# Seven-product SwiGLU in a hybrid decoder layer: weight sums moved to VectorE, rounds overlapped by one product

## The chip, the cores and the metric

The kernel runs on one core of one Trainium2 chip. The metric is the device time of one execution in microseconds, taken as the median of several runs. The engines are named as in the profile: PE is TensorE's matmul, PEld its weight load, DVE is VectorE, ACT is ScalarE, POOL is GpSimd, SP is SyncE, which here only issues DMAs.

## The reference

One decoder layer on 512 tokens of width 1024, in float32: three token mixers (a gated linear recurrence, a chunked gated linear attention, a complex diagonal state space model), merged and projected; cross-attention into 256 memory tokens; a SwiGLU feed-forward of width 2816; a layer norm after each. The change touches the last part:

```
h2 = LN2(alpha * h1 + xattn)
gate, up = split(h2 @ w_gu)               # 1024 x 5632
h3 = LN3(alpha * h2 + (silu(gate) * up) @ w_down)
```

## The kernel before

Every weight product is made in a split form. A block of weights (128x1024, float32) is loaded by SP into a raw tile, copied by ACT to a rounded tile `whi`, and DVE writes the remainder `wlo = raw - whi`. The activations are split likewise into a high and a low part, and `mm3` (L439) runs three matmuls per pair: high by high, high by low, low by high.

All weight blocks stand in one list, `order`, and four functions walk along it. `dma_to` (L251) issues loads, `hi_to` (L303) ACT's copies, `split_to` (L322) DVE's remainders, and `take` (L351) hands the next block to the product. `take` of block i first emits the remainder of block i+3 and ACT's copy of block i+4; loads are emitted with the copy, or up to three blocks ahead where `room` (L341) finds space. These blocks, sums and split halves share a pool of 14 buffers (`W`, tag "w"); a new tile takes a buffer that came free longest ago, and its writer waits on the chip for the last reader of that buffer. Each engine runs its own instructions strictly in the order in which the program emits them; between engines semaphores order the work.

The feed-forward's first product has 22 features of 128 columns. The first four are plain products of gate and up. Of these the first four blocks are begun on tokens 0 to 255 alone (`half_plain`, L1614), since the transposed tiles of tokens 256 to 511 come later from LN2. The other 18 features are made in nine rounds of two features (L1713). A round treats the weights as a 2x2 block matrix (11, 12, 21, 22: halves of the inner dimension by gate and up), the activations as another (halves of the inner dimension by halves of the tokens), and makes the four block products with seven products instead of eight, for which sums of weight blocks (t1 = 12 - 11, t2 = 22 - t1, 22 - 12, t4 = 21 - t2) and sums of activation blocks (s1 to s4) are needed. One `product` (L1701) is 24 matmuls of 256 columns.

`factor` (L263) loads the four blocks of a round and makes the four weight sums on POOL as `dma_to` reaches them. The seven products of a round run in the order 11, 12, s2, s1, s3, s4, 22 (named by their activation block) and collect in three PSUM banks: pb takes 11, then s2 on top, then s3, then 22; pc takes s1, then s4; pa takes 12. Between them ACT copies bank contents out (m1, u2, m5) and DVE adds (m1 += pa, m5 += pb, u2 += pc). The results sg and sh are queued in `late` and split into `act` tiles by `act_split` (L1660).

The activation sums s1 to s4 are made in `h2_T` (L1591), which a token tile of LN2 calls once its transposes are queued: four 128x512 instructions on POOL for each of tiles 2 and 3. LN2's own power (the inverse root, in `ln_apply`, L485) stands in the same POOL queue. `place_s3` (L1691) writes the split s3 over the tokens' block 21 after the second product of the first round.

The down product is `proj_ln` (L1413) on 11 units for each half of the columns. Its residual h2, stored to DRAM before, is loaded again by `load_res` (L1485) with eight DMAs from POOL's queue, ahead of the call; the LN3 parameters follow with four more in its first unit.

Of the kernel before, what the change touches and what calls it, by code (L numbers as in the profile page):

```python
# [9 lines left out]
F32 = mybir.dt.float32  # L10
# [148 lines left out]
def hybrid_kernel(ctx: ExitStack, tc: tile.TileContext, I, out, dbg=None):  # L159
# [80 lines left out]
    add("w_xq", 8)  # L240
    add("w_xo", 8)
    add("w_gu", 2 * NPLAIN)
    for d in range((KF - NPLAIN) // 2):
        for n in range(7):
            order.append(("w_gu", (NPLAIN + 2 * d, n), 1024))
    add("w_dn", KF)
    raws, splits = {}, {}
    blk = {}
# [2 lines left out]
    def dma_to(n):  # L251
        while st["dma"] < min(n, len(order)):
            i = st["dma"]
            st["dma"] += 1
            name, j, size = order[i]
            if type(j) is tuple:
                raws[i] = factor(*j)
                continue
            size = min(size, I[name].shape[2])
            raws[i] = W("raw", F32)  # L260
            SP.dma_start(raws[i][:, :size], I[name][j])

    def factor(f, n):  # L263


        b = blk.setdefault(f, {})

        def load(k):

            h, up = ((0, 0), (0, 1), (1, 1), (1, 0))[k]  # L270
            b[k] = W("raw", F32)
            for e in range(2):
                SP.dma_start(b[k][:, 512 * e:512 * e + 512], I["w_gu"][2 * (f + e) + up][:, 512 * h:512 * h + 512])

        if n == 0:
            load(0)
            return b[0]
        if n == 1:
            load(3)
            return b[3]  # L280
        if n == 2:
            load(1)
            load(2)
            b["t1"], b["t2"] = W("t1", F32), W("t2", F32)
            G.tensor_tensor(b["t1"], b[1], b[0], ALU.subtract)
            G.tensor_tensor(b["t2"], b[2], b["t1"], ALU.subtract)
            del b[0]
            return b["t2"]
        if n == 3:
            return b.pop("t1")  # L290
        if n == 4:
            G.tensor_tensor(b[1], b[2], b[1], ALU.subtract)
            return b.pop(1)
        if n == 5:
            return b.pop(2)
        t = W("t4", F32)
        G.tensor_tensor(t, b[3], b["t2"], ALU.subtract)
        del blk[f]
        return t

# [2 lines left out]
    def hi_to(n):  # L303

        while st["hi"] < min(n, len(order)):
            i = st["hi"]
            dma_to(i + 1)
            st["hi"] += 1
            if i < NK32:
                continue  # L310
            name, _, size = order[i]
            if name == "w_lr":
                pair = W("wlr", F32R)
                p3 = pair[:, :size].rearrange("p (k e c) -> p e k c", e=2, c=16)
                r3 = raws.pop(i)[:, :size // 2].rearrange("p (k c) -> p k c", c=16)
                his[i] = (p3[:, 0], p3[:, 1], r3, pair)
            else:
                hi = W("whi", F32R)
                his[i] = (hi[:, :size], None, raws.pop(i)[:, :size], hi)
            A.activation(his[i][0], his[i][2], AF.Copy)  # L320
# [19 lines left out]

    def room():  # L341

        names = {x.name for b in blk.values() for x in b.values()} | {x.name for x in raws.values()}
        names |= {x[2].name for x in his.values()}
        return 2 * max(keep[0], 1) + 2 * len(splits) + len(his) + len(names) + 2 <= NBUF_W

# [1066 lines left out]
    def proj_ln(name, actT, nk, hres, lnj, outT, final=False, need=None):  # L1413

        nu = nk // 2
        last = min(4, nu)

        def part(pss, un, w, ts, stop):  # L1420
            for kk in range(2):
                k = 2 * un + kk
                if need is not None:
                    need(k)
                for t in ts:
                    mm3(pss[t], actT[k][t] if type(actT[k]) is list else cut(actT[k], ALL, slice(t * P, (t + 1) * P)),
                        cut(w, ALL, slice(kk * 512, kk * 512 + 512)), k == 0, stop and k == nk - 1)

        sts = [S("st", 7) for _ in range(NT)]

        def half(t, c, ps):
            V.scalar_tensor_tensor(hres[t][c], hres[t][c], ALPHA, ps, ALU.mult, ALU.add,
                                   accum_out=sts[t][:, c:c + 1])
            if c == 0:
                ln_first(hres[t][0], sts[t])

        first = [PS("p0") for _ in range(NT)]
        for un in range(nu):
            w = take(name)
            part(first, un, w, range(NT), True)  # L1440
            if un == 0:
                gb = ln_params(lnj)
            slot()
        second = [PS("p1") for _ in range(NT)]
        done = 0
        for un in range(nu - last):
            w = take(name)
            part(second, un, w, range(NT), False)
            if done < NT:
                half(done, 0, first[done])  # L1450
                done += 1
            slot()
        while done < NT:
            half(done, 0, first[done])
            done += 1
        ws = [take(name, min(AHEAD, NPAIR - 1 - un)) for un in range(last)]
        hout, es = [None] * NT, []

        def tile_gen(t):
            h = ln_apply(hres[t], sts[t], gb)  # L1460
            hout[t] = h
            if final:
                for c in range(2):
                    SP.dma_start(out[t * P:(t + 1) * P, c * 512:(c + 1) * 512], h[c])
                return
            yield T, h[0], h[1]
            if callable(outT):
                outT(h, t)
            else:
                ln_T(h, t, outT)  # L1470
            yield 0

        for t in range(NT):
            for un in range(last):
                part(second, nu - last + un, ws[un], [t], True)
                if t == NT - 1:
                    split_to(nxt[0] + min(AHEAD, NPAIR - last + un + 1))
                if un == 0 and t > 1:
                    finish(es[t - 2])
            half(t, 1, second[t])  # L1480
            es.append(start_bg(tile_gen(t)))
            slot()
        return hout, es
# [107 lines left out]
    def h2_T(h, t):  # L1591
        plain[t] = [H("hT0"), H("hT1")]
        for c in range(2):
# [3 lines left out]
            dst = (ALL, ALL, slice(t * P, (t + 1) * P))  # L1597
            split(h2T8[0][c][dst], h2T8[1][c][dst], ps.rearrange("p (k t) -> p k t", t=P))
            A.activation(plain[t][c], ps, AF.Copy)
        if t < 2:  # L1600
            return

        (a11, a12), (a21, a22) = plain[t - 2], plain[t]
        G.tensor_tensor(a22, a21, a22, ALU.add)
        G.tensor_tensor(a21, a11, a21, ALU.subtract)
        G.tensor_tensor(a11, a22, a11, ALU.subtract)
        G.tensor_tensor(a12, a12, a11, ALU.subtract)
        sums[t] = {"s1": a22, "s2": a11, "s3": a21, "s4": a12}

    h2, es = proj_ln("w_xo", oT, KD, h1, 2, h2_T, need=need_head)  # L1610
    finish_all(es[0], es[1])
# [19 lines left out]
        place("s4", part, H("s4", F32R), H("s4", F32R))  # L1631
    for i, (w, ps) in enumerate(pre):
        half_plain(ps, w, 1)
        if i < 3:
            for t in (2, 3):
                n = ("s2", "s1", "s4")[i]
                to_block(n, t, sums[t][n])
        keep[0] -= 1
        split_to(nxt[0] + min(AHEAD, i + 1))
        prefetch(st["split"] + DMA_AHEAD)  # L1640
# [50 lines left out]
    def place_s3():  # L1691
# [1 line left out]
        for part in range(2):  # L1693
            pl["s3", part], wr["s3", part] = pl["21", part], wr["21", part]
        for t in (2, 3):
            to_block("s3", t, sums[t]["s3"])
        sums.clear()
        plain.clear()

# [10 lines left out]
        product(ps, take("w_gu"), n, first)  # L1710
        slot()

    for d in range((KF - NPLAIN) // 2):  # L1713
        pa, pb, pc_ = PS("wa"), PS("wb"), PS("wc")
        m1, m5, u2, sg, sh = H("m1"), H("m5"), H("u2"), H("sg"), H("sh")
        step(pb, "11", True)
        A.activation(m1, pb, AF.Copy)
        step(pa, "12", True)
        V.tensor_tensor(m1, pa, m1, ALU.add)
        A.activation(sg, m1, AF.Silu)  # L1720
        if d == 0:
            place_s3()
        step(pb, "s2")
        A.activation(u2, pb, AF.Copy)
        step(pc_, "s1", True)
        A.activation(m5, pc_, AF.Copy)
        step(pb, "s3")
        V.tensor_tensor(m5, pb, m5, ALU.add)
        step(pc_, "s4")
        V.tensor_tensor(u2, pc_, u2, ALU.add)  # L1730
        V.tensor_tensor(sg, sg, u2, ALU.mult)
        step(pb, "22")
        A.activation(sh, pb, AF.Silu)
        V.tensor_tensor(sh, sh, m5, ALU.mult)
        fs = [NPLAIN + 2 * d, NPLAIN + 2 * d + 1]
        act_tiles(fs, (0, 1), sg)
        act_tiles(fs, (2, 3), sh)
        if len(late) > 9:
            act_split()
        del m1, m5, u2, sg, sh, pa, pb, pc_  # L1740
    pl.clear()
    wr.clear()

# [1 line left out]
        while late and (act[min(k + 6, KF - 1)] is None or None in act[min(k + 6, KF - 1)]):  # L1745
            act_split()

    hres = load_res(h2d)
    hout, es = proj_ln("w_dn", act, KF, hres, 3, None, final=True, need=need_act)
    finish_all(*es)  # L1750
    assert nxt[0] == len(order)
    LOG.append(("life", plan.life))
# [90 lines left out]
```

## Time and profile before

| | |
|---|---|
| median of 3 runs | 1017.77 us (1017.7 to 1022.61) |
| the profiled execution | 1021.16 us, its span 1019.5 us |
| PE busy | 981.0 us, 96% |
| PEld busy | 840.3 us, 82% |
| DVE busy | 633.9 us, 62% |
| ACT busy | 417.1 us, 41% |
| POOL busy | 288.9 us, 28% |
| mean granted clock of TensorE | 0.989 of full |

Times in the rows are microseconds from the span's start, or nanoseconds where a mean or median of one instruction is given. PE's busy time counts pipelined instructions and is not a measure of its peak; what counts here is when it stands idle and where its clock falls. The rounds of the seven-product form run from 687.27 to 891.43 us, the down product follows.

### The profile page before, as it was taken

The page shows a single profiled execution, that of the slowest core. Times are in us where ns is not written, and L with a number is a line of the kernel's source. Part 1 is how long each engine was busy: PE and PEld are TensorE (multiplying, and loading weights), DVE is VectorE, ACT ScalarE, POOL GpSimd, SP SyncE. Part 2 cuts the span into 40 slices and gives each one's busy share as a digit, 9 for nine tenths or more (in the row PEclk, how much of TensorE's full clock was granted, in tenths as well). Part 3 has the DMA queues.
Part 4 walks back from the last instruction along what each step waited for, and adds up shares of the span by engine and source line. Part 5 has one row for each costly group of instructions (what it writes and reads, how often), then busy time and mean ns, then how long its engine had stood idle before and what let it go on. Part 6 is the DMA issues. An engine that isn't in the chain of part 4 may idle for free. (4 is left out here: it accounts for less than half of the span.)

```text
span 1019.5 us, 14088 instructions
## 1 busy us (share of the span) xinstructions
PE 981.0 (96%) x5504; PEld 840.3 (82%) x5504; DVE 633.9 (62%) x935; ACT 417.1 (41%) x672; POOL 288.9 (28%) x325
## 2 busy tenths in 40 slices
PE   9999999999999999999989999899989999799996
PEld 7888778877888888888878887889989899788885
DVE  5725897695686634575854557657777776653316
ACT  5634565523343225533534443444344434442311
POOL 1489950053315010020100001544444454400001
PEclk9999999999999999999989999899999999999998
DMA  9932132324245454372321212142233322632202
GB/s 352 338 124 101 62 118 100 108 84 134 94 126 184 134 165 145 120 237 97 124 83 63 102 63 82 46 142 84 83 111 115 108 83 84 248 125 86 101 21 82
DMA packets 43554, 123.85 MB, mean 121 GB/s; under 512 B 5440, under 2 KB 5856, under 8 KB 43488
## 3 DMA queue, kind: packets, MB, share of 16 engines
q1 hardware_dynamic: 35040, 97.79, 27.8%
q0 software_dynamic: 6592, 22.02, 6.6%
q10 hardware_dynamic: 1856, 3.15, 1.1%
q8 instruction: 43, 0.70, 0.3%
q14 instruction: 23, 0.19, 0.1%
HBM read 109.31 MB, written 11.53 MB: 119 GB/s over the span
## 5 line engine op out<-in xcount | busy, mean ns | idle before, releaser
L75 DVE TENSOR_TENSOR wlo<-raw,whi 128x1024 fp32r<-128x1024 f32 x162 | 206.4, 1282 | 89.8 <-PE p L75 45.6
L75 ACT ACTIVATE whi<-raw 128x1024 fp32r<-128x1024 f32 x162 | 170.0, 1058 | 109.4 <-PE p L75 34.3
L75 PE MATMUL p<-whi,act 128*128 128x512 f32 x352 | 108.6, 389 | 0.0
L75 POOL TENSOR_TENSOR st<-st,mh 128x1 f32<-128x1 f32 x16 | 15.1, 946 | 267.7 <-DVE st L75 267.7
L75 PE MATMUL gt<-h0Th,whi 128*128 128x512 f32 x192 | 79.2, 413 | 0.0
L75 PEld LDWEIGHTS p<-whi,act 128*128 128x128 f32 x352 | 66.1, 188 | 13.7
L75 PE MATMUL gt<-h0Th,wlo 128*128 128x512 f32 x192 | 75.0, 391 | 0.0
L75 PE MATMUL gt<-h0Tl,whi 128*128 128x512 f32 x192 | 74.9, 390 | 0.0
L75 DVE TENSOR_TENSOR wlo<-t,whi 128x1024 fp32r<-128x1024 f32 x27 | 52.2, 1934 | 31.8 <-ACT whi L75 31.8
L75 PE MATMUL wb<-h2Th,whi 128*128 128x256 f32 x216 | 61.9, 287 | 7.9 <-ACT u L75 7.9
L75 PE MATMUL p<-wlo,act 128*128 128x512 f32 x176 | 68.5, 389 | 0.0
L75 PE MATMUL wb<-h2Tl,whi 128*128 128x256 f32 x216 | 61.1, 283 | 0.0
L75 PE MATMUL wb<-h2Th,wlo 128*128 128x256 f32 x216 | 61.1, 283 | 0.0
L75 PE MATMUL wc<-s,whi 128*128 128x256 f32 x288 | 53.9, 287 | 3.7 <-ACT m L75 3.7
L75 ACT ACTIVATE th<-gt,gbh 128x512 f32<-128x512 f32 x24 | 16.6, 692 | 98.4 <-PE gt L75 89.4
L75 POOL TENSOR_TENSOR t<-raw,t 128x1024 f32<-128x1024 f32 x18 | 49.8, 2766 | 21.4 <-issue 14.5
L75 ACT ACTIVATE whi<-t 128x1024 fp32r<-128x1024 f32 x27 | 27.6, 1049 | 63.8 <-POOL t L75 63.8
L75 PEld LDWEIGHTS wb<-h2Th,whi 128*128 128x128 f32 x216 | 41.4, 191 | 9.5 <-ACT u L75 9.5
L75 PEld LDWEIGHTS wc<-s,whi 128*128 128x128 f32 x288 | 45.6, 195 | 3.9 <-ACT m L75 3.9
L75 POOL TENSOR_TENSOR t<-raw,raw 128x1024 f32<-128x1024 f32 x9 | 21.6, 2403 | 91.9 <-DMA raw<-in_w_gu 39.2
L75 PE MATMUL wc<-s,wlo 128*128 128x256 f32 x144 | 41.7, 289 | 1.2 <-DVE wlo L75 1.2
L75 PEld LDWEIGHTS gt<-h0Th,wlo 128*128 128x128 f32 x192 | 36.0, 188 | 7.7
(393 smaller groups left out, 2576.0 us busy)
## 6 DMA issues: line engine op xcount, KB each, us to landing
raw<-in_w_gu SPq DMA_DIRECT2D x72, 256.0 KB, 3.9
raw<-in_w_dn SPq DMA_DIRECT2D x22, 512.0 KB, 3.5
raw<-in_w_xk SPq DMA_DIRECT2D x8, 512.0 KB, 6.7
raw<-in_w_gatea SPq DMA_DIRECT2D x8, 512.0 KB, 3.5
raw<-in_w_gateb SPq DMA_DIRECT2D x8, 512.0 KB, 3.5
raw<-in_w_gatec SPq DMA_DIRECT2D x8, 512.0 KB, 4.3
raw<-in_w_xv SPq DMA_DIRECT2D x8, 512.0 KB, 3.5
raw<-in_w_mix SPq DMA_DIRECT2D x8, 512.0 KB, 3.7
```

The costliest lines, as they stand in the source:

```text
L75: return f(*a, **k)
```

## The change

- The weight sums and the activation sums are made on DVE (`V`) in place of POOL (`G`).
- Loading and summing are parted. `load_blocks` issues the loads when `dma_to` reaches a block; `factor` makes the sums only when `hi_to` reaches it, just ahead of ACT's copy.
- The order of a round becomes 11, 22 of the round before, s2, s1, 12, s3, s4; the last "22" follows the loop (`last_product`). The loads go in the order 11, then 12 and 22 together, then 21. The bank pb and the tile m5 of a round live on into the next.
- The activation sums are no longer made in `h2_T` but by `sum_of`, behind the second halves of the first and third plain blocks.
- `place_s3` stands behind the first product of the first round.
- `act_split` is called in the last four rounds (before: from the third round on, in seven of nine).
- The last residual is loaded inside `proj_ln`, in the second unit of its first half.

```diff
     add("w_gu", 2 * NPLAIN)
-    for d in range((KF - NPLAIN) // 2):
-        for n in range(7):
-            order.append(("w_gu", (NPLAIN + 2 * d, n), 1024))
+    fs = range(NPLAIN, KF, 2)
+    for f in fs:
+        order += [("w_gu", (g, n), 1024) for g, n in ((f, 1), (f - 2, 4), (f, 6), (f, 5), (f, 2), (f, 7), (f, 3))
+                  if g >= NPLAIN]
+    order.append(("w_gu", (fs[-1], 4), 1024))
...
-    def factor(f, n):
+    def load_blocks(f, n):
         b = blk.setdefault(f, {})
+        for k in {1: ("11",), 6: ("12", "22"), 2: ("21",)}.get(n, ()):
             b[k] = W("raw", F32)
+            h, up = int(k[0]) - 1, int(k[1]) - 1
             for e in range(2):
                 SP.dma_start(b[k][:, 512 * e:512 * e + 512], I["w_gu"][2 * (f + e) + up][:, 512 * h:512 * h + 512])
...
+    def factor(f, n):
+        b = blk[f]
+        if n < 4:
+            return b["11" if n == 1 else "21" if n == 2 else "22"]
+        if n == 6:
             b["t1"], b["t2"] = W("t1", F32), W("t2", F32)
-            G.tensor_tensor(b["t1"], b[1], b[0], ALU.subtract)
-            G.tensor_tensor(b["t2"], b[2], b["t1"], ALU.subtract)
+            V.tensor_tensor(b["t1"], b["12"], b["11"], ALU.subtract)
+            V.tensor_tensor(b["t2"], b["22"], b["t1"], ALU.subtract)
...
-            G.tensor_tensor(b[1], b[2], b[1], ALU.subtract)
+            V.tensor_tensor(b["12"], b["22"], b["12"], ALU.subtract)
...
-        G.tensor_tensor(t, b[3], b["t2"], ALU.subtract)
+        V.tensor_tensor(t, b["21"], b["t2"], ALU.subtract)
...
             if un == 0:
                 gb = ln_params(lnj)
+            if un == 1 and callable(hres):
+                hres = hres()
...
-        G.tensor_tensor(a22, a21, a22, ALU.add)
-        G.tensor_tensor(a21, a11, a21, ALU.subtract)
-        G.tensor_tensor(a11, a22, a11, ALU.subtract)
-        G.tensor_tensor(a12, a12, a11, ALU.subtract)
+    def sum_of(n, t):
+        (a11, a12), (a21, a22) = plain[t - 2], plain[t]
+        o, x, y, op = {"s1": (a22, a21, a22, ALU.add), "s3": (a21, a11, a21, ALU.subtract),
+                       "s2": (a11, a22, a11, ALU.subtract), "s4": (a12, a12, a11, ALU.subtract)}[n]
+        V.tensor_tensor(o, x, y, op)
...
+    def last_product(f, pb, m5):
+        step(pb, "22")
+        sh = H("sh")
+        A.activation(sh, pb, AF.Silu)
+        V.tensor_tensor(sh, sh, m5, ALU.mult)
+        act_tiles([f, f + 1], (2, 3), sh)
+
+    before = None
+    for f in range(NPLAIN, KF, 2):
         step(pb, "11", True)
         A.activation(m1, pb, AF.Copy)
-        step(pa, "12", True)
-        V.tensor_tensor(m1, pa, m1, ALU.add)
-        A.activation(sg, m1, AF.Silu)
-        if d == 0:
+        if before is None:
             place_s3()
+        else:
+            last_product(*before)
         step(pb, "s2")
         A.activation(u2, pb, AF.Copy)
         step(pc_, "s1", True)
         A.activation(m5, pc_, AF.Copy)
+        step(pa, "12", True)
+        V.tensor_tensor(m1, pa, m1, ALU.add)
+        A.activation(sg, m1, AF.Silu)
         step(pb, "s3")
         V.tensor_tensor(m5, pb, m5, ALU.add)
         step(pc_, "s4")
...
-        if len(late) > 9:
+        act_tiles([f, f + 1], (0, 1), sg)
+        before = (f, pb, m5)
+        if f >= KF - 8:
             act_split()
...
+    last_product(*before)
...
-    hres = load_res(h2d)
-    hout, es = proj_ln("w_dn", act, KF, hres, 3, None, final=True, need=need_act)
+    hout, es = proj_ln("w_dn", act, KF, lambda: load_res(h2d), 3, None, final=True, need=need_act)
```

## Rows read from the trace of the kernel before

**Rows 1.** The page, its head: the span of the profiled execution.
```profile
span 1019.5 us, 14088 instructions
```

**Rows 2.** Stretches: us, busy of each engine (instructions), PEclk, DMA share, GB/s.
```profile
631.59:652.21 20.62, 14.81 (x113) 13.93 (x111) 13.62 (x22) 7.99 (x13) 6.33 (x5) 0.91 0.30 100
652.21:665.48 13.27, 13.12 (x97) 12.83 (x97) 9.51 (x12) 8.13 (x16) 9.55 (x12) 0.88 0.34 121
687.27:707.30 20.03, 20.03 (x170) 20.03 (x169) 13.90 (x13) 8.20 (x11) 7.32 (x3) 1.00 0.32 106
749.95:772.50 22.55, 20.85 (x171) 20.24 (x170) 16.49 (x13) 10.06 (x13) 10.21 (x5) 1.00 0.29 94
863.00:891.43 28.43, 22.54 (x171) 21.72 (x169) 16.70 (x15) 12.18 (x15) 13.95 (x15) 0.94 0.61 221
687.27:891.43 204.16, 187.44 (x1514) 183.15 (x1512) 146.10 (x116) 89.87 (x115) 91.66 (x45) 0.99 0.34 114
```

**Rows 3.** Waits of PE, 687 to 892 us: waited for, total us, times, longest.
```profile
PE wb L75 <- ACT u L75: 7.9, 8, 1.1
PE wb L75 <- ACT m L75: 4.0, 6, 1.0
PE wc L75 <- ACT m L75: 3.7, 1, 3.7
```

**Rows 4.** The chain of waits, 736 to 760 us: start, us, what.
```profile
740.22 0.33 SPq L75
...
742.49 5.32 DMA raw<-in_w_gu
...
752.99 1.99 DVE wlo L75
```

**Rows 5.** Instructions of single tiles in the loop: duration ns min/median/max, first and last start.
```profile
L75 DVE TENSOR_TENSOR wlo<-raw,whi x37: 1207/1224/3416, 689.5 to 890.1; 128x1024 fp32r<-128x1024 f32 x37
L75 DVE TENSOR_TENSOR wlo<-t,whi x26: 1210/1227/3426, 688.1 to 876.8; 128x1024 fp32r<-128x1024 f32 x26
...
L75 POOL TENSOR_TENSOR t<-raw,t x17: 2407/2733/3264, 690.8 to 869.1; 128x1024 f32<-128x1024 f32 x17
```

**Rows 6.** Groups by form in the loop: busy us, mean ns | idle before, releaser.
```profile
L75 DVE TENSOR_TENSOR wlo<-t,whi 128x1024 fp32r<-128x1024 f32 x26 | 49.9, 1919 | 28.4 <-ACT whi L75 28.4
...
L75 ACT ACTIVATE whi<-raw 128x1024 fp32r<-128x1024 f32 x38 | 40.1, 1056 | 23.0 <-DMA raw<-in_w_gu 10.6 <-DMA raw<-in_w_dn 7.6 <-issue 2.8
...
L75 DVE TENSOR_TENSOR sh<-sh,m 128x512 f32<-128x512 f32 x8 | 5.4, 678 | 0.0
L75 ACT ACTIVATE u<-wb 128x512 f32<-128x512 f32 x9 | 5.2, 577 | 0.0
```

**Rows 7.** The chain of waits at the end of LN2.
```profile
642.95 1.68 POOL hT L75
...
649.00 0.52 POOL st L75
649.54 0.76 DVE lh L75
```

**Rows 8.** The timeline of PE there: start, us, instruction, idle before.
```profile
650.44 1.09 PE L75 MATMUL tp<-ident,lh 128*128 128x128 f32 x4 [4.11 <-DVE lh L75]
```

**Rows 9.** Instructions on the LN statistics, 637 to 660 us.
```profile
L75 DVE TENSOR_TENSOR st<-st x4: 149/702/1267, 642.2 to 644.7; 128x1 f32<-128x1 f32 x4
...
L75 DVE SCALAR_TENSOR_TENSOR st<-st x1: 159/159/159, 646.0 to 646.0; 128x1 f32<-128x1 f32 x1
```

**Rows 10.** The page, DMA issues: KB each, median us to landing.
```profile
raw<-in_w_gu SPq DMA_DIRECT2D x72, 256.0 KB, 3.9
```

**Rows 11.** DMA issues from 860 to 900 us: KB each, median us to landing.
```profile
raw<-in_w_dn SPq DMA_DIRECT2D x8, 512.0 KB, 8.8
res<-h2d POOLq DMA_DIRECT2D x8, 256.0 KB, 6.8
```

**Rows 12.** The residual's first use, from 860 us on.
```profile
L75 DVE SCALAR_TENSOR_TENSOR res<-res,p x7: 679/686/687, 949.5 to 1005.9; 128x512 f32<-128x512 f32 x7
```

More of the change, by code (lines that the diff above doesn't have):

```diff
@@ L256, in dma_to @@
             if type(j) is tuple:
-                raws[i] = factor(*j)
+                load_blocks(*j)
+                raws[i] = None
                 continue
@@ L261, in dma_to @@
             SP.dma_start(raws[i][:, :size], I[name][j])
-    def factor(f, n):
+    def load_blocks(f, n):
         b = blk.setdefault(f, {})
-        def load(k):
-            h, up = ((0, 0), (0, 1), (1, 1), (1, 0))[k]
+        for k in {1: ("11",), 6: ("12", "22"), 2: ("21",)}.get(n, ()):
             b[k] = W("raw", F32)
+            h, up = int(k[0]) - 1, int(k[1]) - 1
             for e in range(2):
                 SP.dma_start(b[k][:, 512 * e:512 * e + 512], I["w_gu"][2 * (f + e) + up][:, 512 * h:512 * h + 512])
[L275 to L283, printed above, removed]
+    def factor(f, n):
[3 more added lines that the diff above has]
+        if n == 6:
             b["t1"], b["t2"] = W("t1", F32), W("t2", F32)
-            G.tensor_tensor(b["t1"], b[1], b[0], ALU.subtract)
-            G.tensor_tensor(b["t2"], b[2], b["t1"], ALU.subtract)
-            del b[0]
+            V.tensor_tensor(b["t1"], b["12"], b["11"], ALU.subtract)
+            V.tensor_tensor(b["t2"], b["22"], b["t1"], ALU.subtract)
+            del b["11"]
             return b["t2"]
-        if n == 3:
+        if n == 5:
             return b.pop("t1")
-        if n == 4:
-            G.tensor_tensor(b[1], b[2], b[1], ALU.subtract)
-            return b.pop(1)
-        if n == 5:
-            return b.pop(2)
+        if n == 7:
+            V.tensor_tensor(b["12"], b["22"], b["12"], ALU.subtract)
+            return b.pop("12")
         t = W("t4", F32)
-        G.tensor_tensor(t, b[3], b["t2"], ALU.subtract)
+        V.tensor_tensor(t, b["21"], b["t2"], ALU.subtract)
         del blk[f]
@@ L310, in hi_to @@
                 continue
-            name, _, size = order[i]
+            name, j, size = order[i]
+            if type(j) is tuple:
+                raws[i] = factor(*j)
             if name == "w_lr":
@@ L341, in room @@
     def room():
-        names = {x.name for b in blk.values() for x in b.values()} | {x.name for x in raws.values()}
+        names = {x.name for x in (*raws.values(), *(t for b in blk.values() for t in b.values())) if x is not None}
         names |= {x[2].name for x in his.values()}
@@ L1599, in h2_T @@
             A.activation(plain[t][c], ps, AF.Copy)
-        if t < 2:
-            return
+    def sum_of(n, t):
         (a11, a12), (a21, a22) = plain[t - 2], plain[t]
-        G.tensor_tensor(a22, a21, a22, ALU.add)
-        G.tensor_tensor(a21, a11, a21, ALU.subtract)
-        G.tensor_tensor(a11, a22, a11, ALU.subtract)
-        G.tensor_tensor(a12, a12, a11, ALU.subtract)
-        sums[t] = {"s1": a22, "s2": a11, "s3": a21, "s4": a12}
+        o, x, y, op = {"s1": (a22, a21, a22, ALU.add), "s3": (a21, a11, a21, ALU.subtract),
+                       "s2": (a11, a22, a11, ALU.subtract), "s4": (a12, a12, a11, ALU.subtract)}[n]
+        V.tensor_tensor(o, x, y, op)
+        sums[n, t] = o
     h2, es = proj_ln("w_xo", oT, KD, h1, 2, h2_T, need=need_head)
@@ L1633, in hybrid_kernel @@
         half_plain(ps, w, 1)
-        if i < 3:
-            for t in (2, 3):
+        for t in (2, 3):
+            for n in (("s1", "s3", "s2"), (), ("s4",), ())[i]:
+                sum_of(n, t)
+            if i < 3:
                 n = ("s2", "s1", "s4")[i]
-                to_block(n, t, sums[t][n])
+                to_block(n, t, sums[n, t])
         keep[0] -= 1
@@ L1695, in place_s3 @@
         for t in (2, 3):
-            to_block("s3", t, sums[t]["s3"])
+            to_block("s3", t, sums["s3", t])
         sums.clear()
@@ L1711, in step @@
         slot()
-    for d in range((KF - NPLAIN) // 2):
+    def last_product(f, pb, m5):
[6 more added lines that the diff above has]
+    for f in range(NPLAIN, KF, 2):
         pa, pb, pc_ = PS("wa"), PS("wb"), PS("wc")
-        m1, m5, u2, sg, sh = H("m1"), H("m5"), H("u2"), H("sg"), H("sh")
+        m1, m5, u2, sg = H("m1"), H("m5"), H("u2"), H("sg")
         step(pb, "11", True)
         A.activation(m1, pb, AF.Copy)
-        step(pa, "12", True)
-        V.tensor_tensor(m1, pa, m1, ALU.add)
-        A.activation(sg, m1, AF.Silu)
-        if d == 0:
+        if before is None:
             place_s3()
+        else:
+            last_product(*before)
         step(pb, "s2")
@@ L1731, in hybrid_kernel @@
         V.tensor_tensor(sg, sg, u2, ALU.mult)
[L1732 to L1737, printed above, removed]
-        if len(late) > 9:
+        act_tiles([f, f + 1], (0, 1), sg)
+        before = (f, pb, m5)
+        if f >= KF - 8:
             act_split()
-        del m1, m5, u2, sg, sh, pa, pb, pc_
+    last_product(*before)
     pl.clear()
```

## The prediction

> **What bounds the kernel now.** I read the page first: the span is 1019.5 us [rows 1], and TensorE is busy nearly all of it, so every microsecond to win is one in which TensorE stands still or runs at its lower clock. The table of stretches [rows 2] says where that is. The loop of the seven-product form lasts 204.16 us (687.27 to 891.43). Its first round takes 20.03 us with TensorE never idle, which is 2.86 us for each of the seven products. Nine such rounds would be 180.3 us, so 23.9 us of the loop are lost; the last round alone takes 28.43 us, at a granted clock of 0.94. The second place is the end of LN2: 631.59 to 652.21 and the stretch after it, with clocks of 0.91 and 0.88.
>
> TensorE's waits in the loop [rows 3] name ACT copies out of PSUM. But the chain [rows 4] shows what makes ACT late: at 740.22 SyncE begins a burst of issues (the last of six at 742.49), that DMA takes 5.32 us, GpSimd's sums follow, and only at 752.99 does DVE get to the split. One such turn per round is longer than 20.03 us. GpSimd also slows DVE. A wlo split takes 1.22 us in the median, but up to 3.42 [rows 5], and the group on summed blocks has a mean of 1919 ns [rows 6], because its instructions fall on GpSimd sums of 2.4 to 3.3 us.
>
> **LN2, sums to DVE.** The chain [rows 7] shows the first of four GpSimd sums of tile 2 at 642.95 and the tiny power of tile 3, queued behind them, at 649.00. TensorE's transposes start at 650.44 after 4.11 us of idle, so it ran dry at 646.3 [rows 8]. Beside the sums a 128x1 DVE instruction took up to 1.27 us where 0.15 is its least; tile 3's last such one starts at 646.0 [rows 9]. Without two such delays of 1.1 the statistics are through at about 644.0, the power and the first lh take 0.52 and 0.76, and the transposes are fed at about 645.5, before TensorE runs dry. So the idle 4.1 us goes. The following 96 products of 256 columns took 13.27 us [rows 2] at clock 0.88; at the 2.86/24 = 0.119 us of the loop they take 11.4, which gives back 1.85. What is late next is the transposed tile's own split (ACT copy, then DVE), about 1 us of TensorE. I count 5.5 us gained (bounds 2 and 6.8). The eight sums are now 8 x 0.68 [rows 6] = 5.4 us of DVE. They stand between tile 3's split and the weight splits of the third plain feature, covered by four half products (11.4 us); if the cover fails it costs up to 2 us, hence the lower bound.
>
> **The loop, sums to DVE.** Per round, GpSimd's four sums go and DVE gets four. The trace has no such sum on DVE; the nearest row has the same shape and operands, the wlo split: 1.21 us undisturbed, 3.42 at worst [rows 5]. I take the median of 1.22, as no GpSimd arithmetic is left to stand in its way. DVE per round: 7 splits and 4 sums x 1.22 = 13.4, five evacuations x 0.68 = 3.4, together 16.8 of 20.03 us, with one act split (0.68) more in the last four rounds. That fits, but DVE is in order, so I follow its turn.
>
> **The loop, reordered.** Time 0 is the end of product "12"; s3, s4, the next "11" and "22" end at 2.86, 5.72, 8.58 and 11.44. Blocks 12 and 22 go into the two weight buffers that came free longest ago. I take them to be those of "12" itself, freed at 0. Four issues at 0.45 us (six between 740.22 and 742.49 [rows 4]) and 3.9 us to landing [rows 10] put block 12 there at 4.4 and block 22 at 5.3. DVE: t1 at 4.4 to 5.6, t2 to 6.8, the m5 add to 7.5; "22" accumulates on that bank at 8.58, so 1.1 us are spare. ACT splits t2 by 7.9 (1.06), DVE by 9.1; "s2" needs it at 11.44. Then u2 and sg (1.4), two splits and a sum (3.7), ACT's whi and silu (1.6), sh (0.7), three splits and the t4 sum (4.9): 21.4, that is 1.4 into the next turn. Its split is done at about 4.3, just before the next t1 at 4.4. The ring closes with almost nothing to spare, yet it closes at TensorE's pace.
>
> The three stalls of [rows 3]: "wb after u" (8 times, 7.9 us) and "wb after m" (6 times, 4.0) are the same bank used again with the copy (577 ns) in between. Now "22" of the previous round lies between "11" and "s2", and s1 and "12" between "s2" and s3: 2.86 us or more cover 0.58, so they go if ACT isn't itself blocked by a whi in front. "wc after m" (3.7) belongs to the hand-over below. One PSUM bank more is held over a round's edge, four of eight.
>
> **The residual.** In the last round eight residual loads (256 KB, 6.8 us to landing) and the LN parameters are issued right behind GpSimd's last sum, and the first w_dn blocks take 8.8 us [rows 11]; TensorE stops 3.7 us for a copy queued behind such a block's whi [rows 3]. Moved to the second unit of w_dn, the eight issues stand behind the four parameter loads on GpSimd's queue, which now holds nothing else, so these may even go earlier. First need: 949.5 [rows 12], over 50 us of cover. The hand-over's 28.43 should become about 22, at full clock.
>
> I leave 4 us in the loop: 1 for the first round (block s3's split now between "11" and "s2", first loads), 2 for the hand-over, 1 for the rounds. So the loop gains 23.9 - 4 = 19.9.
>
> **Sum.** The profiled execution took 1021.16 us: 1021.16 - 19.9 - 5.5 = 995.8. It lies 3.4 above the median of 1017.77, so I forecast 992 for a median. The floor, with every loss at both places gone (23.9 + 6.8), is 987; the low end of 985 allows for the spread of medians.
>
> **Rivals.**
> (a) DVE's ring is the bound. If blocks 12 and 22 get the buffers of the t4 sum's operands, the turn runs: two blocks landed 5.3 after t4, t2 1.2, whi and wlo 2.3, then 1.4 + 3.7 + 1.6 + 0.7 + 4.9 = 21.0. That is 1 us a round over eight rounds: 1000. For it: DVE at 84%. Against: t4 is planned late in the order.
> The Trainium skill (Perfetto Trace Analysis, Optimizing Scalar/DVE Operations) advises the reverse move when DVE is saturated, offloading to other engines, even GpSimd, with the warning that the two share a read port. The rows bear out the warning (1.22 against 3.42); no run here yet shows a saturated DVE.
> (b) The gaps are those of the fourteen weight buffers, whose number stays. Then rounds stay at about 22.55 [rows 2], and only LN2 (5.5) and the hand-over (28.43 - 22.55 = 5.9) are won: 1006. For it: the chain goes through SyncE waiting for buffers. Against: the burst is now four issues, not eight, and GpSimd's 5 us are out of it.
> The Trainium skill (Perfetto Trace Analysis, Optimization Strategy) reads a gap that repeats on the engine that should be saturated as possibly too little room for the next tile; by that the time would be that of (b).
> (c) Block 21's load gets a buffer that only product "11" frees. ACT's whi of it stands in front of the m1 copy: 0.45 + 3.9 + 1.06 + 0.58 = 6.0 after "11", while "s2" could start at 2.86. That is 3.1 us a round, 25 in all: 1017, no change.
> (d) Slower. The wait for blocks 12 and 22 stands on DVE in front of the m5 add, and "22" waits for that add. The point is 1.1 us after "12": from a buffer that is free at the end of s4 (5.72) the add ends at 13.2, 4.6 late, 37 us in eight rounds: 1029. For it: DVE in order, fourteen buffers all full at that step. Against: five other buffers come free earlier by my count.
>
> **How the numbers follow.** Forecast 992 with 0.60 (988 to 998 its own range), (a) 0.16, (b) 0.10, (c) 0.07, (d) 0.07. A measurement of this kernel tells about 0.5% (5 us) from no change. Faster: 0.60 + 0.16 + 0.10 = 0.86; same: 0.07; slower: 0.07. The range 985 to 1012 holds the first three, from the floor on, with (b) a little worse than worked out.
>
> **What would show it.** Right: the loop 183 to 187 us, rounds from the second on at 20.0 to 20.4, wlo means near 1.22 everywhere, GpSimd without 128x1024 sums, no 4 us idle before the transposes of tile 3, w_dn's first landings below 5 us. (a): DVE gapless, TensorE waiting for wlo. (b): SyncE waiting, DVE waiting for DMAs of w_gu, rounds of 22. (c): "s2" waiting for the m copy. (d): "22" waiting for DVE's m5 add. Wrong at LN2: the transposes put into TensorE's queue so early that it stops for lh.

## The result and the profile after

The changed kernel takes 995.43 us, the median of 4 runs (993.32 to 996.75), against 1019.83 us for the kernel before (4 runs, 1017.7 to 1022.61). The ratio is 0.9757, with a 95% interval of 0.9722 to 0.9792. The forecast was 992 in a range of 985 to 1012.

The profiled execution took 993.32 us, its span 991.6 us, and lies 2.1 us under its median. These are stretches of it: us, then the busy time of PE, PEld, DVE, ACT and POOL with their instructions, the granted clock, the DMA share and GB/s. The first two rows answer to the two LN2 stretches of [rows 2], the next three are the first, the second and the last round (the last with both its closing products), then the whole loop and what follows it.

```profile
630.23:646.13 15.90, 13.93 (x113) 13.20 (x111) 10.42 (x22) 7.99 (x13) 3.40 (x6) 1.00 0.45 157
646.13:658.75 12.62, 12.13 (x96) 11.73 (x97) 10.36 (x17) 5.13 (x10) 1.85 (x4) 1.00 0.59 215
680.54:699.82 19.28, 17.41 (x145) 17.20 (x144) 11.89 (x13) 7.25 (x10) 0.00 (x0) 1.00 0.25 82
699.82:719.85 20.03, 20.03 (x170) 20.03 (x169) 16.00 (x16) 9.66 (x12) 0.00 (x0) 1.00 0.32 106
840.05:863.60 23.55, 23.41 (x194) 23.01 (x193) 19.09 (x22) 13.58 (x17) 4.05 (x8) 1.00 0.49 175
680.54:863.60 183.06, 181.05 (x1513) 180.44 (x1512) 144.56 (x148) 89.13 (x113) 6.24 (x12) 1.00 0.36 118
863.60:991.00 127.40, 119.87 (x530) 98.95 (x528) 56.95 (x104) 35.46 (x54) 3.98 (x5) 0.99 0.27 96
```

The loop lasts 183.06 us in place of 204.16, which is 21.1 us gained. The two LN2 stretches last 28.52 in place of 33.89, 5.4 gained. The rest up to the span's 27.9 us are 1.4 us ahead of LN2's end, in code that the change leaves alone. The down product takes 128 us in both.

TensorE's waits in the loop (waited for, total us, times, longest), where [rows 3] had three rows with 15.6 us:

```profile
PE wb L75 <- ACT m L75: 1.9, 1, 1.9
```

One wait is left, in the first round. VectorE's groups in the loop (busy us, mean ns, then idle time before and what ended it) answer to [rows 5, 6]:

```profile
L75 DVE TENSOR_TENSOR wlo<-raw,whi 128x1024 fp32r<-128x1024 f32 x38 | 45.5, 1219 | 7.1 <-ACT whi L75 6.9
L75 DVE TENSOR_TENSOR wlo<-t,whi 128x1024 fp32r<-128x1024 f32 x25 | 30.6, 1223 | 10.6 <-ACT whi L75 10.6
L75 DVE TENSOR_TENSOR t<-raw,t 128x1024 f32<-128x1024 f32 x17 | 20.8, 1221 | 3.4 <-DMA raw<-in_w_gu 3.4
```

The mean is now the same for all three; the middle group had 1919 ns. The sum that the trace of before couldn't show costs 1221 ns on VectorE.

Now one turn of VectorE, in two views: the chain of waits (here TensorE alone; start, us, what), and VectorE's timeline.

```profile
751.46 2.87 PE wa L75 x24
754.32 2.88 PE wb L75 x24
...
760.08 8.59 PE wb L75 x72
...
```

```profile
758.51 1.22 DVE L75 TENSOR_TENSOR t<-raw,raw 128x1024 f32<-128x1024 f32 x1
759.77 1.23 DVE L75 TENSOR_TENSOR t<-raw,t 128x1024 f32<-128x1024 f32 x1
760.91 0.69 DVE L75 TENSOR_TENSOR m<-wb,m 128x512 f32<-128x512 f32 x1
762.20 1.22 DVE L75 TENSOR_TENSOR wlo<-t,whi 128x1024 fp32r<-128x1024 f32 x1 [0.61 <-ACT whi L75]
...
774.22 1.22 DVE L75 TENSOR_TENSOR t<-raw,t 128x1024 f32<-128x1024 f32 x1
```

Product "12" ends at 754.32; that is time 0 of the forecast's turn. The rows put the start of t1 at 4.2 (forecast 4.4), the end of the m5 add at 7.3 (7.5), t2's split done at 9.1 (9.1), t4 done at 21.1 (21.4).

### The profile page after: what moved, and what is told of

Its sections match the earlier page's. It is cut to its first block, busy times and chain, and to the rows that moved or that the text cites. A ratio compares the mean times of both kernels' runs of the same rounds, so it can differ in the third digit from the quotient of the medians.

```text
span 991.6 us, 14008 instructions
## 1 busy us (share of the span) xinstructions
PE 971.2 (98%) x5504; PEld 834.7 (84%) x5504; DVE 634.2 (64%) x979; ACT 418.0 (42%) x672; POOL 184.7 (19%) x281
## 5 line engine op out<-in xcount | busy, mean ns | idle before, releaser
L75 DVE TENSOR_TENSOR wlo<-raw,whi 128x1024 fp32r<-128x1024 f32 x162 | 197.7, 1233 | 81.7 <-PE p L75 44.1
L75 POOL DMA_DIRECT2D lnp<-in_lnp x12 | 6.5, 548 | 236.9 <-ACT sg L75 170.6
L75 PEld LDWEIGHTS wb<-h2Tl,whi 128*128 128x128 f32 x216 | 41.5, 192 | 0.0
L75 PEld LDWEIGHTS wb<-h2Th,wlo 128*128 128x128 f32 x216 | 41.5, 192 | 0.0
L75 PEld LDWEIGHTS gt<-h0Th,whi 128*128 128x128 f32 x192 | 36.2, 189 | 5.8 <-issue 0.2
```

The costliest lines, as they stand in the source:

```text
L75: return f(*a, **k)
```

## The experiments

Days and chips differ by a few us, so kernels are compared by their ratio to the kernel before, run alongside; 0.001 is 1 us. The changed kernel's is 0.9757.

**e1 and e2: the engine of the weight sums, and the order of the products, each alone.**

e1, in `factor` (22 - 12 and t4 likewise):

```diff
-            V.tensor_tensor(b["t1"], b["12"], b["11"], ALU.subtract)
-            V.tensor_tensor(b["t2"], b["22"], b["t1"], ALU.subtract)
+            G.tensor_tensor(b["t1"], b["12"], b["11"], ALU.subtract)
+            G.tensor_tensor(b["t2"], b["22"], b["t1"], ALU.subtract)
```

> The changed kernel with its four weight sums per round back on GpSimd, at the same places in the order; everything else stays. Theory E (the engine of the sums wins the loop): a sum takes 2.4 to 2.7 us on GpSimd against 1.22 on VectorE, so t2 is 2.7 us later, while the split for product s2 has 2.0 to 2.6 us to spare in the changed kernel, and splits beside a GpSimd sum take up to 3.4 us; 1 to 2.5 us lost per round in eight rounds, 1003 to 1015 us, I take 1008. Rival O (the order of the products wins it, whoever sums): within 2 us of the changed kernel's 995.4 us.

Measured: 1016.01 us, ratio 0.9929 (0.9898 to 0.996), 17.5 us lost against the changed kernel: theory E, at the far end of what it gave. The ten runs spread from 1003.56 to 1019.88, wider than any other kernel's; why is left open. The chain of waits shows a turn:

```profile
799.55 2.89 DVE sh L75
802.44 1.15 DVE wlo L75
...
804.01 4.36 DMA raw<-in_w_gu
...
813.13 3.28 POOL t L75
...
816.44 1.07 ACT whi L75
```

GpSimd's timeline there has the first of the two sums (in brackets its idle time before):

```profile
809.83 3.23 POOL L75 TENSOR_TENSOR t<-raw,raw 128x1024 f32<-128x1024 f32 x1 [7.94 <-DMA raw<-in_w_gu]
```

Read it as a ring: a VectorE product of 2.89 us (0.68 undisturbed) delays a split, the split frees a buffer, and a burst of loads goes out (the one shown takes 4.36 us). GpSimd's first sum waits for a later load of that burst, the second (813.13) follows it at once, then comes ScalarE's copy. The chain itself reaches the second sum through a product of TensorE that ends at the same time as the first sum, within 0.1 us. It is the ring of [rows 4]. The loop lasts 204.48 us against 204.16 before: with the sums on GpSimd the new order gains nothing. TensorE's two largest waits in this loop:

```profile
PE wb L75 <- ACT m L75: 11.4, 7, 2.3
PE wc L75 <- ACT m L75: 7.8, 6, 2.3
```

e2, the order (the steps of the loop follow it, each round closing with its own "22"):

```diff
-        order += [("w_gu", (g, n), 1024) for g, n in ((f, 1), (f - 2, 4), (f, 6), (f, 5), (f, 2), (f, 7), (f, 3))
-                  if g >= NPLAIN]
-    order.append(("w_gu", (fs[-1], 4), 1024))
+        order += [("w_gu", (f, n), 1024) for n in (1, 2, 6, 5, 7, 3, 4)]
```

> The changed kernel with the products of a round in the order of before (11, 12, s2, s1, s3, s4, 22, no overlap of rounds); sums on VectorE, late residual and activation splits as in the changed kernel. Theory E (with the sums on VectorE, ScalarE's copies out of PSUM are no longer late): no stall per round above 0.4 us, 995 to 1001 us, I take 998. Rival O (the stalls after the u and m copies belong to the order, because the same PSUM bank is used again with one product between): they come back at their old sum of 7.9 + 4.0 us, 1007 us.

Measured: 1001.15 us, ratio 0.9812 (0.9791 to 0.9833): 5.6 us lost, between the two theories. The stretch of its loop, and TensorE's waits there:

```profile
680.87:870.39 189.52, 182.72 (x1514) 180.89 (x1513) 145.24 (x147) 88.65 (x112) 6.38 (x12) 1.00 0.34 116
```

```profile
PE wb L75 <- ACT m L75: 5.1, 8, 1.0
PE wb L75 <- ACT u L75: 1.6, 1, 1.6
```

Of the two stalls of [rows 3], the one after u is gone but for one of 1.6 us (7.9 before): without late sums the old order has it no more. It doesn't occur in e1 either, so each of the two moves alone removes it; in e1 the late sums then stop TensorE after the m copies, for 11.4 and 7.8 us. The stall after m stays in e2 (4.0 before): with the sums on VectorE it belongs to the order. The chain shows why:

```profile
810.58 1.23 DVE raw L75
...
811.83 0.02 ACT whi L75
...
812.79 0.59 ACT m L75
...
813.43 3.10 PE wb L75 x24
```

VectorE's sum 22 - 12 holds ScalarE's whi, and the m copy is queued behind it. In the new order "22" lies between "11" and "s2" and covers it.

The four loops together: old order with GpSimd 204.16, new order with GpSimd 204.48, old order with VectorE 189.52, new order with VectorE 183.06. The engine is worth 14.6 to 21.4 us, the order nothing or 6.5. The kernel before differs from the other three in more than these two (where its sums are emitted, its activation splits, its residual loads), so the two differences from it, 14.6 and nothing, aren't of engine or order alone.

**e3 and e4: the activation sums, engine and place apart.** e3 puts `G` for `V` in `sum_of`; e4 calls it from `h2_T`:

```diff
             A.activation(plain[t][c], ps, AF.Copy)
+        if t > 1:
+            for n in ("s1", "s3", "s2", "s4"):
+                sum_of(n, t)
...
-            for n in (("s1", "s3", "s2"), (), ("s4",), ())[i]:
-                sum_of(n, t)
```

> The changed kernel with the eight activation sums on GpSimd, but at their new place behind the second half products. Theory P (the 4.1 us idle before tile 3's transposes came from the place: sums ahead of tile 3's power in GpSimd's queue): tile 3's transposes still follow without idle time; the six sums of s1, s3, s2 at 1.68 us make the splits behind them on VectorE late by some 2 us against the first full-width gate product: 996 to 999 us, I take 997.5. Rival (GpSimd beside VectorE slows the LN statistics themselves, wherever the sums stand): the idle time before tile 3's transposes is back, about 4 us, and with the lower clock behind it 1001 us.

> The changed kernel with the eight activation sums on VectorE, but queued where before had them, right behind each tile's transposes in LN2. Theory P (the place counts): tile 2's four sums (4 x 0.68 = 2.7 us) stand on VectorE ahead of tile 3's statistics, of which some 1 us falls into VectorE's idle time: tile 3's transposes wait 1.5 to 2.7 us, 997 to 998.5 us. Rival (only the engine counts): no idle time before tile 3's transposes, 995.4 us.

Measured: e3 998.13 us, ratio 0.9783 (0.9763 to 0.9802), as expected in time but not in kind; e4 1000.66 us, ratio 0.9815 (0.9787 to 0.9842), more lost than expected. Four fences: TensorE's wait in e3 and the row of VectorE's timeline behind it, then the wait in e4 and, in VectorE's timeline, the sums ahead of tile 3's statistics:

```profile
PE tp L75 <- DVE lh L75: 1.6, 2, 1.0
```

```profile
646.31 3.45 DVE L75 SCALAR_TENSOR_TENSOR lh<-lt,st,lnp 128x512 f32<-128x512 f32 x2 [0.44 <-POOL st L75]
```

```profile
PE tp L75 <- DVE lh L75: 3.2, 1, 3.2
```

```profile
641.79 2.87 DVE L75 TENSOR_TENSOR hT<-hT,hT 128x512 f32<-128x512 f32 x4 [0.66 <-ACT hT L75]
644.58 0.15 DVE L75 TENSOR_TENSOR st<-st 128x1 f32<-128x1 f32 x1
```

Both theories hold in part. Behind the power, GpSimd's sums no longer delay it, but the two lh instructions beside them take 3.45 us (1.41 in the changed kernel), and the transposes wait 1.6. On VectorE but at the old place, the four sums and their wait for a ScalarE copy cost 3.2 of the 4.11 us of [rows 8]. In e4 the mean granted clock is also 0.96 from 648.42 to 690 us, behind that stall, against 1.00 in the changed kernel; how much of the 5.9 us lost that makes is left open. The whole gain needs the other engine and the later place.

**e5 and e6: the residual.** e5 passes `load_res(h2d)` in place of the lambda to the changed kernel; e6 makes the late load alone, in the kernel before:

```diff
             if un == 0:
                 gb = ln_params(lnj)
+            if un == 1 and callable(hres):
+                hres = hres()
...
-    hres = load_res(h2d)
-    hout, es = proj_ln("w_dn", act, KF, hres, 3, None, final=True, need=need_act)
+    hout, es = proj_ln("w_dn", act, KF, lambda: load_res(h2d), 3, None, final=True, need=need_act)
```

> The changed kernel with the eight residual loads issued ahead of the down product again, as before had them. Theory R (the residual's 2 MB compete with the first blocks of w_dn): w_dn's first blocks land in 8 us or so in place of 3.5, ScalarE and then TensorE wait for them at the hand-over; 2 to 5.9 us lost, 997.5 to 1001.5 us, I take 999. Rival (the transfer is hidden, and the 3.7 us stall of before came from late sums): 995.4 us.

> The kernel before with one part of the change alone: the residual loaded in the second unit of the down product. Theory R: the stall of 3.7 us at the hand-over goes and most of the 5.9 us by which the last round is longer than its neighbours: 4 to 6 us faster than before, ratio 0.994 to 0.996. Rival (hidden anyway): ratio 1.000.

Measured: e5 996.13 us, ratio 0.9749 (0.9727 to 0.9771); e6 1022.75 us, ratio 1.0011 (0.9995 to 1.0026). By time the rival holds in both: where the program calls for the residual makes no difference that can be measured. In e6 the stall at the hand-over is still there, 4.1 us. First the chain, then GpSimd's timeline beside it:

```profile
874.34 1.22 DVE wlo L75
...
875.58 8.30 DMA raw<-in_w_dn
...
883.97 1.06 ACT whi L75
885.02 0.49 ACT m L75
...
885.56 4.63 PE wc L75 x24
```

```profile
875.47 2.73 POOL L75 DMA_DIRECT2D res<-h2d  x5
```

The w_dn load goes out only when a split on VectorE, late behind GpSimd's sums, frees its buffer. It takes 8.30 us, and five residual loads are issued beside it from 875.47 us on, a sixth at 878.38: the later call put them behind the four LN parameter loads (from 873.28 us on), but not out of the way. So e6 shows what the call is worth, not what the residual's traffic costs.

In the changed kernel too the residual loads fall among the first w_dn loads, which begin at 852.61 us:

```profile
851.70 1.08 POOL L75 DMA_DIRECT2D res<-h2d  x2 [19.36 <-DVE sh L75]
859.53 2.69 POOL L75 DMA_DIRECT2D res<-h2d  x5 [6.75 <-ACT sg L75]
```

The first four w_dn loads take 5.0 to 7.0 us there. In e5 the residual's are issued from 772.42 to 813.68 us, ahead of all of w_dn, and the first four w_dn loads take 5.9 to 7.8 us. In neither does TensorE wait for a copy behind them.

**e7 and e8: how thin VectorE's turn is.** The sum t1, or t1 and t2, made twice (the second time with the same result):

```diff
             V.tensor_tensor(b["t1"], b["12"], b["11"], ALU.subtract)
+            V.tensor_tensor(b["t1"], b["12"], b["11"], ALU.subtract)
```

> The changed kernel with the sum t1 made twice in each round: 1.13 us more for VectorE, all of it ahead of the m5 add. Theory Q (VectorE's queue ahead of the m5 add decides; in the changed kernel the add ends 0.7 to 1.2 us before product 22 starts): nearly all of the spare time used, 0 to 0.4 us lost per round, 995.5 to 998.5 us, I take 997. Rival S (only VectorE's busy share counts, now 16.05 of 20.03 us): 995.4 us.

> The changed kernel with t1 and t2 made twice in each round: 2.3 us more for VectorE ahead of the m5 add. Theory Q: the add ends 1.1 to 1.6 us after the time at which product 22 could start, lost in each of eight rounds: 1004 to 1008 us, I take 1006. Rival S (VectorE is then busy for 18.4 of 20.03 us, still under a round): 995.4 us.

Measured: e7 1000.0 us, ratio 0.9778 (0.9748 to 0.9809), 2.1 us lost, which by time alone can't be told from nothing (its loop lasts 187.65 us, 4.6 more than the changed kernel's); e8 1010.07 us, ratio 0.9886 (0.9861 to 0.991), 12.9 lost. e8 decides for theory Q, with slightly more lost than the theory gave. TensorE's waits in e8's loop, and one of them in its timeline (in brackets the idle time before):

```profile
PE wb L75 <- DVE m L75: 10.1, 9, 1.6
```

```profile
770.03 0.36 PE L75 MATMUL wb<-h2Th,whi 128*128 128x256 f32 x1 [1.15 <-DVE m L75]
```

This is product "22" waiting for the m5 add. VectorE is busy for 163.90 of the loop's 197.01 us there, 83%. Its busy share isn't the limit; its queue ahead of one add is.

**e9: the buffers.** `NBUF_W = 13` in place of 14.

> The changed kernel with thirteen weight buffers in place of fourteen. Theory Q (fourteen are enough; what is thin is the time ahead of the m5 add): some 21 buffers are taken per round of 20 us, so each load is issued about 1 us later, which the 0.7 to 1.2 us of spare time of the m5 add just about hold: 995.5 to 999 us, I take 998. Rival B (the number of buffers sets the pace of the rounds): a round loses 2 us or more, as in the kernel before, 1011 us or more.

Measured: 996.46 us, ratio 0.9762 (0.9736 to 0.9787). No round is slower than in the changed kernel by more than 0.4 us; 2.4 us are lost at the last "22" alone. The fourteen buffers don't set the pace of the rounds.

**e10 and e11: GpSimd at work beside VectorE.** e10 adds arithmetic that nothing needs; e11 puts 22 - 12 and t4 back on GpSimd (`G` for `V` in these two lines of `factor`), t1 and t2 not.

```diff
         A.activation(m5, pc_, AF.Copy)
+        gs = H("gs")
+        G.tensor_tensor(gs, m5, m5, ALU.subtract)
+        for _ in range(5):
+            G.tensor_tensor(gs, gs, gs, ALU.subtract)
+        del gs
```

> The changed kernel with idle arithmetic added on GpSimd: once per round, after the m5 copy, six 128x512 subtractions on a tile of their own (9 to 10 us per round), on which nothing waits. Theory N (GpSimd at work beside VectorE slows it): t1, t2, the m5 add and the split of t2 fall beside it and take up to 2.2 us more each, the add is 2 to 4 us late in eight rounds, 1009 to 1025 us, I take 1014. Rival (only the lateness of the sums themselves counted in the kernel before): within 2 us of the changed kernel, ratio 0.976.

> The changed kernel with two of its four weight sums per round on GpSimd (22 - 12, and t4), t1 and t2 staying on VectorE: VectorE is relieved by 2.4 us per round. Theory N: the sum 22 - 12 runs beside the m5 add and the split of t2 and makes the two up to 2.2 us longer, 0.5 to 1.5 us lost per round: 999 to 1007 us, I take 1003. Rival (VectorE's load is what is thin, so sharing helps or costs nothing): 993 to 996 us.

Measured: e10 1010.86 us, ratio 0.9906 (0.9881 to 0.993), 15 us lost, as theory N has it. e11 992.21 us, ratio 0.9724 (0.9696 to 0.9753): theory N fails, and this is the fastest kernel of the study, though its interval overlaps the changed kernel's. First VectorE's groups in e10, then VectorE's timeline in e11, with GpSimd's own row last:

```profile
L75 DVE TENSOR_TENSOR t<-raw,t 128x1024 f32<-128x1024 f32 x16 | 32.1, 2006 | 0.3
L75 DVE TENSOR_TENSOR t<-raw,raw 128x1024 f32<-128x1024 f32 x8 | 16.5, 2057 | 0.0
L75 DVE TENSOR_TENSOR m<-wb,m 128x512 f32<-128x512 f32 x8 | 5.4, 678 | 0.0
```

```profile
758.46 0.68 DVE L75 TENSOR_TENSOR m<-wb,m 128x512 f32<-128x512 f32 x1
759.73 2.17 DVE L75 TENSOR_TENSOR wlo<-t,whi 128x1024 fp32r<-128x1024 f32 x1 [0.58 <-ACT whi L75]
...
757.50 3.32 POOL L75 TENSOR_TENSOR raw<-raw,raw 128x1024 f32<-128x1024 f32 x1 [6.49 <-DVE t L75]
```

In e10 t1 and t2 fall beside GpSimd and take 2.0 us each, and TensorE waits 13.2 us for the m5 add. In e11 GpSimd's sum falls beside the m5 add, which isn't slowed (0.68), and one split, which has time to spare. VectorE is relieved, and the add ends 1.9 to 3.6 us before "22" starts in the eight rounds, against 0.7 to 1.2. So what costs is GpSimd in the ring (e1), or beside the sums ahead of the m5 add (e10), and not GpSimd at work as such.

**e12: the first round.** The stall that is left comes from VectorE: it waits for the last plain feature's up product before it makes the sum 22 - 12, whose copy ScalarE has in front of the m1 copy. ScalarE's timeline in the changed kernel:

```profile
683.85 1.06 ACT L75 ACTIVATE whi<-raw 128x1024 fp32r<-128x1024 f32 x1 [4.77 <-DVE raw L75]
684.81 0.58 ACT L75 ACTIVATE m<-wb 128x512 f32<-128x512 f32 x1
```

The idle 4.77 us ahead of whi are the wait for that sum. The edit emits one block's copies and sums earlier:

```diff
+        if f == NPLAIN - 1:
+            hi_to(nxt[0] + AHEAD + EARLY + 1)
         V.tensor_tensor(s, s, pre[1], ALU.mult)
```

> The changed kernel with one thing more: before VectorE waits for the last plain feature's up product, ScalarE's copies and the sums of one block further ahead are emitted, so that the sum 22 - 12 of the first round and the copy behind it no longer stand behind that wait and in front of the m1 copy. Theory: the 1.87 us idle before s2 in the first round goes, ratio 0.974, about 1.9 us faster than the changed kernel. Rival: the copies ahead take weight buffers that the next loads need, and the gap moves on: no change, ratio 0.976.

Measured: 993.81 us, ratio 0.9737 (0.9716 to 0.9758). The stall shrinks from 1.87 to 0.69 us, the loop from 183.06 to 182.47. By time it can't be told from the changed kernel; e11's loop takes 181.51, with the same shorter stall.

## Why the prediction was right, and where it was not

**The loop** was forecast to gain 19.9 us and gained 21.1. The mechanism is the one forecast: the ring through sums, splits, buffers and loads closes within TensorE's 20.03 us once t1 and t2 take 1.22 us. The costs in it that were only bounded came out at the end chosen: the sum 1.22 (bounds 1.21 and 3.42), splits 1.22; VectorE's round takes 16.0 us (forecast 16.8). Of the 4 us left over, the first round took 2.1 (19.28 less six products of 2.86; forecast 1), the hand-over 0.7 (23.55 less eight; forecast 2), the rounds between nothing (forecast 1). That the loop came out so close is in part luck, as these misses partly cancel.

**The stalls.** "They go if ACT isn't itself blocked": they went. But it gave both stalls to the order alone. u's goes with the sums alone as well (e2); only m's needs the order, and the order alone doesn't remove it (e1).

**The residual** is the step that failed. The prediction said that the eight residual loads beside w_dn's first blocks stopped TensorE for 3.7 us, and that the later call takes them out of the way. On the chip they stayed: in the changed kernel all eight are issued from 851.70 to 863.33 us, among the first w_dn loads. Its sign, "w_dn's first landings below 5 us", didn't come (5.0 to 7.0), and still TensorE doesn't wait. The call alone gains nothing (e6), and without it nothing is lost (e5). The stall went with another part of the change: in e2, with the sums on VectorE and the old order, the first w_dn load goes out at 856.76 us, lands 3.5 us later, and TensorE doesn't wait for a copy behind it. In the kernel before it went out late, at 874.59, and took 7.87 us beside residual loads, LN parameters and other w_dn loads. How much of these 7.87 us the residual cost there stays open, since e6 didn't take it away. The term was gained, but not by the step that was to gain it: that is luck.

**LN2** was forecast to gain 5.5 and gained 5.4, of which 4.7 in its first stretch and 0.65 in its second. The idle 4.1 us went, at both its causes (e3, e4). The granted clock was 1.00 in the second stretch, the upper level of 2.4 GHz, against 0.88 (before, it stood at 0.50, the lower level of 1.2 GHz, from 648.6 to 655.3 us, after TensorE had run dry at 646.3). Yet the 96 products took 12.62 us, not 11.4: short waits for the transposed tile's split, the "about 1 us" that the prediction named as late next but took off only in part (4.11 + 1.85 - 5.5 = 0.46).

**The sum.** 1021.16 - 19.9 - 5.5 = 995.8 was for a profiled execution; it came in at 993.32, 1.4 of it from ahead of LN2's end, where the clock from 500 us on was 0.99 against 0.97. Subtracting 3.4 for the median was the wrong term: before's profiled execution lay above its median, which is 1019.83 us with a fourth run in place of 1017.77, and after's lay below.

**The rivals.** (a), VectorE's ring as the bound, fell: TensorE never waits for wlo. (b), buffers, fell: the rounds last 20.03 us with the same fourteen, and thirteen do as well (e9). (c), ScalarE's whi in front of the m1 copy, happens once, in the first round (1.9 us). (d), "22" late behind the m5 add, didn't occur, but its point was right: 1.1 us to spare were worked out, the eight rounds show 0.7 to 1.2, and e8, with 2.3 us more ahead of the add, lost 1.0 to 1.6 in seven of eight.

## What to carry to other kernels

When an engine's sums sit in a ring of loads, buffers and splits, count the ring's turn, not busy shares: moving the two sums ahead of the m5 add decided, and the other two could as well stay on GpSimd (e11). Separate edits that go in together by undoing each, and then look in the trace at what the undoing did on the chip: a load that the program calls for later (e6) still went out beside the one that it was to make way for. When work leaves one engine, look which single instruction on the next one now has the least time to spare.

## What the hardware showed

A GpSimd subtraction beside VectorE does not slow all of VectorE's instructions alike. In e10 t1 and t2, with both inputs in SBUF, took 2.0 us in place of 1.22; the m5 add, with one input in PSUM, kept 0.68. The Trainium skill (SBUF — State Buffer, Who interferes with whom) says just that: a VectorE instruction with two SBUF inputs meets a GpSimd instruction that reads SBUF, one with at most one SBUF input does not. The trace agrees (2.0 against 0.68).

GpSimd slowed as well: of its 128x512 subtractions there the shortest took 1.04 us, half of them 1.90 or more. The last row of the three is VectorE's t1, beside the second:

```profile
L75 POOL TENSOR_TENSOR gs<-gs x38: 1040/1902/1908, 698.6 to 858.2; 128x512 f32<-128x512 f32 x38
764.68 1.90 POOL L75 TENSOR_TENSOR gs<-gs 128x512 f32<-128x512 f32 x1
765.61 2.06 DVE L75 TENSOR_TENSOR t<-raw,raw 128x1024 f32<-128x1024 f32 x1
```

This GpSimd subtraction ends at 766.58, 0.97 us after t1's start, and t1 ends 1.09 us after that; the next GpSimd subtraction (766.66, 1.90 us) ends 0.89 us after t1. The two take turns rather than share. The same section of the Trainium skill lets the second comer stand still until the first is through; the trace agrees, as far as GpSimd's spans can be relied on, since t1's 2.06 us are those 0.97 us beside the subtraction, near the 1.04 us of the shortest, and then 1.09 us.
